# Moving each pair's last product behind two products of the next pair, in a decoder trunk on one Trainium2 core

## The chip, the core and the metric

The kernel runs on one NeuronCore of a Trainium2 chip. TensorE (PE) multiplies matrices: a weight load (PEld) puts 128x128 weights in place, a matmul then streams up to 512 columns past them, and the sums go to a bank of PSUM. VectorE (DVE) and ScalarE (ACT) do elementwise work, GpSimd (POOL) and SyncE (SP) here mostly start DMA transfers. Each engine works through its own instructions in order and waits for others by semaphores. The metric is the device time of one execution in microseconds (us); the time before is 2514.36 us, the median of 3 runs.

## What is computed

The reference is a trunk of two layers on 1024 rows of 1024 channels in float32. Each layer has a mixer (a state-space mixer in the first, an SSD mixer in the second) and a squared-ReLU MLP; the change lies in the MLPs alone.

```python
def _sq_relu_mlp(h, w1, w2):
    a = jax.nn.relu(h @ w1)
    return (a * a) @ w2

def reference(x, c, ...):
    cond = jax.nn.silu(c)
    for i in range(DEPTH):
        mod = cond @ ada_w[i] + ada_b[i]
        sh1, sc1, g1, sh2, sc2, g2 = jnp.split(mod[:, None, :], N_MOD, axis=-1)
        h = _modulate(_rmsnorm(x, norm_mix_g[i]), sh1, sc1)
        ...
        x = x + g1 * y
        h = _modulate(_rmsnorm(x, norm_mlp_g[i]), sh2, sc2)
        x = x + g2 * _sq_relu_mlp(h, mlp_w1[i], mlp_w2[i])
    return _rmsnorm(x, final_norm_g)
```

## The kernel before

**Precision.** Every float32 product is made of three matmuls. `split` (line 82) rounds a tile to a high part on ACT (line 84) and takes the rest on DVE (line 85). `mm3` (line 112) then issues high times high (line 117), high times low (118) and low times high (119). The split parts of weights are the tiles `whi` and `wlo`; `a` is those of one special tile, `a22`.

**First products (h @ w1).** They are done by a Strassen-like scheme with seven products of half the size. The 4096 outputs of w1 are taken as 16 pairs of 128-wide blocks (`of_pair`, line 457). The activations h lie split in seven panels: `b11`, `b21`, `b22`, `t1`, `t2`, `t3`, `t4`. In the trace the panel shows by the moving operand: `h0` to `h3` are `b11` or, with a trailing half of 1, `t1`; `h4` to `h7` are `b21` or `b22`; `t2`, `t3`, `t4` carry their names. One call of `product` (line 480) multiplies half a weight tile with a panel: four blocks of three matmuls, so 12 matmuls of 512 columns.

For 14 of the 16 pairs (`UPS`) two products, with `b11` and `b21`, are done ahead by `early` (line 515) while the panels for the rest are being made. Their results go to scratch in memory, `sscr` and `cscr`. The last two pairs do these two in place (`g.u0`).

**What one pair does.** `rows` (line 526) loads two raw weight tiles (line 95), splits the half of one into `a22`, forms four sums of halves in place (lines 534 to 537), and splits the two results into the units u1 and u2. `pair` (line 542) then runs, in the program's order:

- the loads of s and b12 from scratch (lines 554, 555);
- product `t2` with u1 into bank X, and `held` (line 490): s2 = s + X on DVE;
- product `t3` with u2 into bank W, and `held`: s7 = s + W;
- `ahead()`, which is `rows` of the next pair;
- product `t1` with u2, added in X; `act` (lines 497, 499, 500): b21 = relu(s7 + X)^2, and `put` stores it by a POOL DMA (line 506);
- product `t4` with `a22`, added in W; b22 = relu(s2 + W)^2, stored; `minus` (line 511) forms and stores t3;
- product `b22` with u1, added in X, the pair's last product; b11 = relu(s + X)^2, stored; then the three differences t1, t2, t4, stored.

**Buffers.** Temporaries of 512 columns (`tmp`, line 73: s, b12, s2, s7 and others) share six buffers. Raw weights share four (the pool `K.raw`; the gate's modulation rows, line 334, take from the same four in the first MLP). Split weights go round a ring of five (`unit_ring`, line 1473). `a22` has two, X four PSUM banks by turns, W three. `tt`, the result of `minus`, has four.

**What sets the order.** The program is written through a tile framework that places the semaphore waits and plans the order of each engine's instructions when the program is built; an earlier place in the program gives precedence. The trace therefore shows an order near the program's but not the same: matmuls of a later pair appear between products of an earlier one.

The loop over the pairs is in `mlp` (lines 1469 to 1497). It also advances `gates`, which in the first MLP computes the rows of one modulation (lines 333 and 334) at pairs 4 to 11. Behind the loop `mlp_down` (line 584) does the second products, whose first bank loads and splits are already planned among the last pairs.

Of the kernel before, what the change touches and what calls it, by code (L numbers as in the profile page):

```python
# [11 lines left out]
F32 = mybir.dt.float32  # L12
F32R = mybir.dt.float32r
I32 = mybir.dt.int32
AF = mybir.ActivationFunctionType
# [4 lines left out]
P = 128  # L20
D = 1024
L = 1024
HT = 512
# [3 lines left out]
UPS = 14  # L27
# [35 lines left out]

def psum(K):

    K.turn += 1
    i = K.turn % (6 if K.wide else 4)
    if i >= 4:
        return K.pw.tile([P, 512], F32, tag="pw", name="pd")
    return (K.ps if i < 2 or not K.psb else K.psb).tile([P, 512], F32, tag="ps", name="pd")  # L70


def psw(K):

    return K.pw.tile([P, 512], F32, tag="pw", name="pm")


def tmp(K, name):
    return K.tmp.tile([P, 512], F32, tag="t", bufs=6, name=name)


def split(K, hi, lo, src):

    K.nc.scalar.copy(hi, src)  # L84
    K.nc.vector.tensor_tensor(lo, src, hi.bitcast(F32), op=ALU.subtract)  # L85


def unit(K, src, n=1024):

    return unit_of(K, unit_raw(K, src, n), n)  # L90


def unit_raw(K, src, n=1024):
    raw = K.raw.tile([P, 1024], F32, tag="raw", name="raw")[:, 0:n]
    K.nc.sync.dma_start(raw, src)
    return raw


def unit_of(K, raw, n=1024):
    K.wturn = (K.wturn + 1) % len(K.wring)  # L100
    wt = K.wring[K.wturn]
    hi = wt.tile([P, 1024], F32R, tag="whi", name="whi")[:, 0:n]
    lo = wt.tile([P, 1024], F32R, tag="wlo", name="wlo")[:, 0:n]
    split(K, hi, lo, raw)
    return hi, lo


def unit_ring(K, *pools):

    K.wring, K.wturn = list(pools), -1  # L110
# [142 lines left out]
def h_new():  # L253
    return [[None, None] for _ in range(KT)]


def x_tiles(pool, order=range(KT)):
    x = h_new()
    for k in order:
        for f in range(2):  # L260
            x[k][f] = pool.tile([P, HT], F32, tag=f"x{k}{f}", name=f"x{k}{f}")
    return x
# [15 lines left out]
def drain(gen):  # L278
    for _ in gen:
        pass  # L280
# [56 lines left out]
def columns(K, rows, n):  # L337

    nc = K.nc
    row = K.wt.tile([P, 1024], F32, tag="whi", name="row")  # L340
    for f, r in enumerate(rows):
        nc.scalar.copy(row[0:1, half_of(f)], r[0:1])
    pt = pss(K)
    for j in range(n):
        nc.tensor.matmul(pt[:, j:j + 1], row[0:1, blk(j)], K.ones[0:1], start=True, stop=True)
    return pt
# [35 lines left out]
def modv(K, i, j):  # L382
    return K.mod[:, i * 48 + j * 8:i * 48 + j * 8 + 8]
# [73 lines left out]
def of_pair(m):  # L457

    i = m // 2 * 4 + m % 2
    return i, i + 2  # L460


class Up:
# [51 lines left out]
    def early(self, m, pan):  # L515

        nc = self.K.nc
        u0 = unit(self.K, self.w1[of_pair(m)[0]])
        X, Z = self.bank(m), self.second_bank()
        self.product(X, u0, 0, pan.b11, True)  # L520
        s1 = self.held(X, "s1")
        nc.gpsimd.dma_start(self.sscr[m], s1)
        self.product(Z, u0, HT, pan.b21, True)
        nc.gpsimd.dma_start(self.cscr[m], self.act(self.held(Z, "s1z", s1), None, True))

    def rows(self, m, pool, late):

        K, V, g = self.K, self.K.nc.vector, SimpleNamespace()
        r0, r1 = [unit_raw(K, self.w1[i]) for i in of_pair(m)]
        g.u0 = unit_of(K, r0) if late else None  # L530
        a22 = pool.tile([P, 1024], F32R, tag="br", name="a22", bufs=2)
        g.a22 = a22[:, 0:HT], a22[:, HT:]
        split(K, *g.a22, r1[:, HT:])
        V.tensor_tensor(r1[:, HT:], r1[:, 0:HT], r1[:, HT:], op=ALU.add)
        V.tensor_tensor(r1[:, 0:HT], r0[:, 0:HT], r1[:, 0:HT], op=ALU.subtract)
        V.tensor_tensor(r0[:, 0:HT], r1[:, HT:], r0[:, 0:HT], op=ALU.subtract)
        V.tensor_tensor(r0[:, HT:], r0[:, HT:], r0[:, 0:HT], op=ALU.subtract)
        g.u1 = unit_of(K, r0)
        g.u2 = unit_of(K, r1)
        return g  # L540

    def pair(self, m, g, pan, ahead):

        K = self.K
        X = self.bank(m)
        if g.u0:
            s = None
            self.product(X, g.u0, 0, pan.b11, True)
            b12 = self.held(X, "s1")
            Z = self.second_bank()  # L550
            self.product(Z, g.u0, HT, pan.b21, True)
        else:
            s, b12 = tmp(K, "s"), tmp(K, "b12")
            K.nc.sync.dma_start(s, self.sscr[m])
            K.nc.sync.dma_start(b12, self.cscr[m])
        self.product(X, g.u1, 0, pan.t2, not g.u0)
        s2 = self.held(X, "s2", s)
        W = self.second_bank()
        self.product(W, g.u2, 0, pan.t3, True)
        s7 = self.held(W, "s7", s)  # L560
        if g.u0:
            self.act(b12, Z)
        ahead()
        self.product(X, g.u2, HT, pan.t1, False)
        b21 = self.act(s7, X, not g.u0)
        self.put("b21", m, b21)
        self.product(W, g.a22, 0, pan.t4, False)
        b22 = self.act(s2, W, not g.u0)
        self.put("b22", m, b22)
        self.minus("t3", m, b22, b12)  # L570
        self.product(X, g.u1, HT, pan.b22, False)
        if s is None:
            b11 = tmp(K, "r")
            K.nc.scalar.activation(b11, X, AF.Relu)
            self.act(b11)
        else:
            b11 = self.act(s, X, True)
        self.put("b11", m, b11)
        t1 = self.minus("t1", m, b12, b11, b12)
        t2 = self.minus("t2", m, b22, t1)  # L580
        self.minus("t4", m, b21, t2)


def mlp_down(K, pool, x, bscr, w2, gate, xscr, mid, extra):
# [442 lines left out]
def s5_uproj(K, h, w):  # L1027

    nc = K.nc
    ahead = unit(K, w[0])  # L1030
    for m in range(KT):
        u = ahead
        if m < KT - 1:
            ahead = unit(K, w[m + 1])
        us = K.raw.tile([P, 1024], F32, tag="raw", name="us").rearrange("p (s c) -> p s c", s=8)
        for f in range(2):
            p = project(K, u, h, f)
            nc.scalar.copy(us[:, :, blk(f, 64)], p.rearrange("p (c s) -> p s c", s=8))
            if f == 0:
                yield  # L1040
        nc.scalar.dma_start(K.uscr[m], us)
        yield
# [385 lines left out]
def trunk(ctx: ExitStack, tc: tile.TileContext, io, out):  # L1428
    nc = tc.nc
    K = SimpleNamespace(nc=nc, tc=tc, io=io, turn=-1, psb=None, wide=False, adap=None, nada=2, nact=7)  # L1430
# [29 lines left out]
    def right(name, n=1):  # L1460
        return tc.alloc_tile_pool(name=name, bufs=n, side="right", reuse_waits="tile")
# [4 lines left out]
    def left(name, n=1):  # L1466
        return tc.alloc_tile_pool(name=name, bufs=n, reuse_waits="tile")

    def mlp(i, x, xa, up, pan, gate, mid, cond=None, mods=(), gates=()):

        mods, gates = iter(mods), iter(gates)
        K.wz = right("wz" + str(i), 2)
        unit_ring(K, K.wt, K.wt, K.wy, K.wz, K.wz)
        for t in ("whi", "wlo"):
            K.wz.tile([P, 1024], F32R, tag=t, name=t, bufs=2)
        rows = up.rows(0, K.wz, False)
        K.to = right("to" + str(i))
        for m in range(16):
            ahead = []
            up.pair(m, rows, pan, lambda: m < 15 and ahead.append(up.rows(m + 1, K.wz, m + 1 >= UPS)))  # L1480
            rows = ahead and ahead[0]
            if m >= 4:
                next(gates, None)
        K.to.release()
        K.tp.release()
        xl = left("xl" + str(i))
        x = x_tiles(xl)
        K.br = right("br" + str(i))
        K.adap = K.br if cond else None
        mlp_down(  # L1490
            K, K.br, x, K.bscr[i], io.w2[i], gate, K.hscr[i], lambda *a: mid(x, *a), lambda: next(mods, None)
        )
        drain(mods)
        K.adap = None
        K.br.release()
        K.wz.release()
        xl.release()
# [51 lines left out]
    g = h_new()  # L1549
    up = s5_uproj(K, h, io.s5_w_in)  # L1550
# [71 lines left out]
    up, mid = entry(0, x, K.G[:, 8:16], modv(K, 0, 3))  # L1622
# [11 lines left out]
    def mid(x, f, bank, order):  # L1634
        G, sh = K.G[:, 16:24], modv(K, 1, 0)

        def each(k, pb):
            h1[k][f] = (h_tile(K, k, f, 0), h_tile(K, k, f, 1))
            norm_tile(K, x[k][f], h1[k][f], pb, G[:, k:k + 1], sh[:, k:k + 1])
            nc.gpsimd.dma_start(K.rscr[k, :, half_of(f)], x[k][f])  # L1640

        return norm_steps(K, x, f, each, bank, order)

    mlp(0, x, xa, up, up.pan, modv(K, 0, 5), mid, True, mod1, gate0)
    cond.release()
    K.wx = left("wx1", 2)
# [8 lines left out]
    t1 = right("tab1")  # L1655
# [24 lines left out]
    up, mid = entry(1, x1, K.G[:, 24:32], modv(K, 1, 3))  # L1680
# [126 lines left out]
```

## Time and profile before

| what | us |
|---|---|
| median of 3 runs (2514.31 to 2516.89) | 2514.36 |
| span of the profiled execution | 2516.1 |
| PE busy in the span | 2445.6 |
| DVE busy in the span | 1913.1 |
| first MLP: from the first product t2 of pair 0 to the end of the pairs | 529 to 775 |
| second MLP: the same | 1942 to 2188 |

The page of the profile gives busy time by engine, the chain that ended last (the work that led to the end, followed back from releaser to releaser) and the costliest groups. Views of the trace give the same for a stretch: busy time by stretch, waits by pairs of engines and lines, the chain piece by piece, and single instructions in order of time. In those rows "px" is bank X of a pair, "pv" is bank W or the bank of an early product, and a bracket says how long the engine was idle before the instruction and what ended it.

### The profile page before, as it was taken

How to read it: one execution, taken by the hardware profiler on the slowest of the kernel's cores; microseconds unless marked ns; L12 is line 12 of the kernel's file. 1: busy time of each engine (PE TensorE's matmuls, PEld its weight loads, DVE VectorE, ACT ScalarE, POOL GpSimd, SP SyncE). 2: the span in 40 equal slices, each digit the busy share in tenths (PEclk: the TensorE clock that was granted, in tenths of full speed). 3: DMA queues.
4: the chain of work that ended last, by engine and by line, in shares of the span. 5: the costliest groups of instructions: out<-in, count | busy, mean ns of one | idle time of the engine just before them, and what ended most of it. 6: DMA issues, size and time to landing. Idle time of an engine off the chain costs nothing.

```text
span 2516.1 us, 32759 instructions
## 1 busy us (share of the span) xinstructions
PE 2445.6 (97%) x11624; PEld 1961.2 (78%) x11624; DVE 1913.1 (76%) x3265; ACT 1167.4 (46%) x1975; POOL 214.4 (9%) x400
## 2 busy tenths in 40 slices
PE   7999899999999999999999999999999999999997
PEld 3788788877777778877887878877888777788886
DVE  8798754978887898968585867789687777787664
ACT  4577412744444334534464645534246444444342
POOL 0010000122221000100000000000011222210000
PEclk8999999999999999999999999999999999999998
DMA  6576773467769999823554554574246666794752
GB/s 244 149 174 165 237 251 97 148 205 258 263 226 318 322 307 320 276 85 109 162 160 153 159 168 145 180 249 141 80 137 210 217 223 222 256 318 150 252 191 84
DMA packets 284643, 503.80 MB, mean 200 GB/s; under 512 B 22080, under 2 KB 162368, under 8 KB 284480
## 3 DMA queue, kind: packets, MB, share of 16 engines
q1 hardware_dynamic: 242496, 386.34, 47.8%
q0 software_dynamic: 32384, 106.98, 12.5%
q10 hardware_dynamic: 9600, 8.39, 1.0%
q8 instruction: 91, 1.49, 0.2%
q14 instruction: 72, 0.59, 0.1%
HBM read 364.27 MB, written 133.17 MB: 198 GB/s over the span
## 4 chain that ended last, share of the span: by engine, by line
PE 80%; DVE 7%; DMA 5%; ACT 3%; issue 2%; DVEq 0%; SPq 0%; ACTq 0%
PE pd L117 11%; PE pd L118 11%; PE pd L119 11%; PE py L117 4%; PE py L119 4%; PE py L118 4%; PE px L117 4%; PE px L119 3%; PE px L118 3%; PE pv L117 3%; PE pv L118 3%; PE pv L119 3%; PE pm L119 2%; PE pm L117 2%; PE pm L118 2%
## 5 line engine op out<-in xcount | busy, mean ns | idle before, releaser
L84 ACT CAST whi<-raw 128x1024 fp32r<-128x1024 f32 x241 | 251.0, 1047 | 360.5 <-PE pd L118 145.4
L85 DVE TENSOR_TENSOR wlo<-raw,whi 128x1024 fp32r<-128x1024 f32 x241 | 293.0, 1217 | 107.8 <-ACT whi L84 104.2
L334 DVE SCALAR_TENSOR_TENSOR ada<-ada,cond 128x1024 f32<-128x1024 f32 x88 | 107.0, 1220 | 57.6 <-DMA ada<-in_ada 57.3
L499 ACT ACTIVATE s<-s 128x512 f32<-128x512 f32 x84 | 53.0, 631 | 156.1 <-DVE s L497 153.6
L391 POOL DMA_DIRECT2D hscr<-x x32 | 17.4, 543 | 955.4 <-DVE x L758 752.5
L1257 DVE SCALAR_TENSOR_TENSOR cacc<-cr,conv,cacc 128x1024 f32<-128x1024 f32 x72 | 91.7, 1277 | 1.0 <-ACT cacc L1238 0.6
L1310 ACT ACTIVATE L<-csb,cs 128x128 f32<-128x128 f32 x224 | 69.9, 390 | 39.8 <-DMA csb<-csr 39.8
L506 POOL DMA_DIRECT2D b<-s x96 | 52.0, 542 | 319.9 <-ACT s L500 278.5
L497 DVE TENSOR_TENSOR s<-s,px 128x512 f32<-128x512 f32 x60 | 41.0, 683 | 34.4 <-PE px L119 34.4
L497 DVE TENSOR_TENSOR s<-s,pv 128x512 f32<-128x512 f32 x36 | 24.7, 686 | 55.1 <-PE pv L119 55.1
L506 POOL DMA_DIRECT2D b<-tt x96 | 52.0, 542 | 44.8 <-DVE tt L511 27.9
L500 ACT ACTIVATE s<-s 128x512 f32<-128x512 f32 x84 | 53.2, 633 | 2.7
L1261 ACT ACTIVATE cth<-cacc 128x512 f32<-128x512 f32 x48 | 27.7, 624 | 42.3 <-DVE cacc L1257 40.4
L673 DVE SCALAR_TENSOR_TENSOR x<-py,mod,x 128x512 f32<-128x512 f32 x40 | 27.6, 743 | 24.4 <-PE py L119 24.4
L209 ACT ACTIVATE sq<-x 128x512 f32<-128x512 f32 x28 | 16.7, 625 | 54.1 <-DVE x L673 49.1
L1330 DVE SCALAR_TENSOR_TENSOR y<-xs,cst,pm 128x128 f32<-128x128 f32 x128 | 38.2, 340 | 4.7 <-PE pm L1327 4.7
L117 PE MATMUL pd<-h00h,whi 128*128 128x512 f32 (+1 forms) x97 | 39.9, 413 | 1.8 <-ACT h00h L238 1.8
L1237 ACT COPY cr<-pd 128x512 f32<-128x512 f32 x48 | 27.8, 579 | 28.8 <-PE pd L119 28.8
L1128 ACT ACTIVATE gt<-pd,bgh 128x512 f32<-128x512 f32 x16 | 11.0, 685 | 63.9 <-PE pd L119 63.9
L117 PE MATMUL pd<-h01h,whi 128*128 128x512 f32 x97 | 39.5, 407 | 0.5 <-DVE h61h L758 0.5
L119 PE MATMUL pd<-h10h,wlo 128*128 128x512 f32 (+1 forms) x97 | 39.3, 405 | 0.0
L118 PE MATMUL pd<-h30l,whi 128*128 128x512 f32 (+1 forms) x97 | 38.9, 401 | 0.0
(1006 smaller groups left out, 8165.1 us busy)
## 6 DMA issues: line engine op xcount, KB each, us to landing
raw<-in_w SPq DMA_DIRECT2D x204, 512.0 KB, 4.7
br<-b SPq DMA_DIRECT2D x112, 512.0 KB, 5.4
ada<-in_ada SPq DMA_DIRECT2D x96, 512.0 KB, 5.3
b<-s POOLq DMA_DIRECT2D x96, 256.0 KB, 2.9
b<-tt POOLq DMA_DIRECT2D x96, 256.0 KB, 3.8
csb<-csr SPq DMA_DIRECT2D x32, 512.0 KB, 4.6
raw<-in_w_xbc SPq DMA_DIRECT2D x24, 512.0 KB, 4.3
xscr<-cacc SPq DMA_DIRECT2D x24, 512.0 KB, 2.7
```

The costliest lines, as they stand in the source:

```text
L84: K.nc.scalar.copy(hi, src)
L85: K.nc.vector.tensor_tensor(lo, src, hi.bitcast(F32), op=ALU.subtract)
L117: K.nc.tensor.matmul(ps, wh, xh, start=start and i == 0, stop=False, skip_group_check=more)
L118: K.nc.tensor.matmul(ps, wh, xl, start=False, stop=False, skip_group_check=more)
L119: K.nc.tensor.matmul(ps, wl, xh, start=False, stop=stop and i == n - 1, skip_group_check=more)
L334: K.nc.vector.scalar_tensor_tensor(r, r, 1.0, K.cond, op0=ALU.mult, op1=ALU.mult, accum_out=acc)
L497: nc.vector.tensor_tensor(t, t, p, op=ALU.add)
L499: nc.scalar.activation(t, t, AF.Relu)
L500: nc.scalar.activation(t, t, AF.Square)
L506: self.K.nc.gpsimd.dma_start(self.bscr[DOWN.index(nm)][m // 2][m % 2], t)
L1257: V.scalar_tensor_tensor(acc, cr[:, t:t + L], K.cw[:, i, t:t + 1], acc, op0=ALU.mult, op1=ALU.add)
L1310: nc.scalar.activation(Lm[:, r, :], cb[:, r, :], AF.Relu, bias=S.cs[:, c0 + r:c0 + r + 1], scale=-1.0)
```

## The change

The work of a pair is cut into `sums`, `units`, `begin`, `middle`, `last` and `finish`, and the loop runs 17 times, with the pair `now`, the pair before it, `done`, and the pair behind it, `ahead`:

- the raw loads, the split of `a22` and the sums of `ahead` stand at the head (for the last two pairs also the split of u0);
- then `begin` of `now`: products `t2` and `t3`, with s loaded before them;
- then `last` of `done`: its product `b22`;
- then the splits u1, u2 of `ahead`, then `finish` of `done`: b11, t1, t2, t4;
- then `middle` of `now`: the load of b12, products `t1` and `t4`, b21, b22 and t3.

The tile b12 that is loaded, and the tile r of the last two pairs, come from two buffers of their own in the pool `K.to`, and no longer from the six temporaries. In the last two pairs the bank of the product `b21` is taken before the product `b11` is issued.

```diff
-    def rows(self, m, pool, late):
+    def sums(self, m, pool, late):
 
-        K, V, g = self.K, self.K.nc.vector, SimpleNamespace()
-        r0, r1 = [unit_raw(K, self.w1[i]) for i in of_pair(m)]
+        K, V, g = self.K, self.K.nc.vector, SimpleNamespace(m=m)
+        r0, r1 = g.raws = [unit_raw(K, self.w1[i]) for i in of_pair(m)]
         g.u0 = unit_of(K, r0) if late else None
...
         V.tensor_tensor(r0[:, HT:], r0[:, HT:], r0[:, 0:HT], op=ALU.subtract)
-        g.u1 = unit_of(K, r0)
-        g.u2 = unit_of(K, r1)
         return g
+    def units(self, g):
+
+        g.u1 = unit_of(self.K, g.raws[0])
+        g.u2 = unit_of(self.K, g.raws[1])
+
+    def begin(self, g, pan):
+
+        K, m = self.K, g.m
+        g.X = self.bank(m)
         if g.u0:
-            s = None
-            self.product(X, g.u0, 0, pan.b11, True)
-            b12 = self.held(X, "s1")
-            Z = self.second_bank()
+            g.s, Z = None, self.second_bank()
+            self.product(g.X, g.u0, 0, pan.b11, True)
+            g.b12 = self.held(g.X, "s1")
             self.product(Z, g.u0, HT, pan.b21, True)
         else:
-            s, b12 = tmp(K, "s"), tmp(K, "b12")
-            K.nc.sync.dma_start(s, self.sscr[m])
-            K.nc.sync.dma_start(b12, self.cscr[m])
+            g.s = tmp(K, "s")
+            K.nc.sync.dma_start(g.s, self.sscr[m])
...
+    def middle(self, g, pan):
+
+        K, m = self.K, g.m
+        if not g.u0:
+            g.b12 = self.K.to.tile([P, HT], F32, tag="b12", name="b12", bufs=2)
+            K.nc.sync.dma_start(g.b12, self.cscr[m])
+        self.product(g.X, g.u2, HT, pan.t1, False)
+        g.b21 = self.act(g.s7, g.X, not g.u0)
+        self.put("b21", m, g.b21)
+        self.product(g.W, g.a22, 0, pan.t4, False)
+        g.b22 = self.act(g.s2, g.W, not g.u0)
+        self.put("b22", m, g.b22)
+        self.minus("t3", m, g.b22, g.b12)
+
+    def last(self, g, pan):
+
+        self.product(g.X, g.u1, HT, pan.b22, False)
+
+    def finish(self, g):
+
+        K, m = self.K, g.m
+        if g.s is None:
+            b11 = K.to.tile([P, HT], F32, tag="b12", name="r", bufs=2)
+            K.nc.scalar.activation(b11, g.X, AF.Relu)
             self.act(b11)
         else:
-            b11 = self.act(s, X, True)
+            b11 = self.act(g.s, g.X, True)
...
-        for m in range(16):
-            ahead = []
-            up.pair(m, rows, pan, lambda: m < 15 and ahead.append(up.rows(m + 1, K.wz, m + 1 >= UPS)))
-            rows = ahead and ahead[0]
+        for m in range(17):
+            ahead = up.sums(m + 1, K.wz, m + 1 >= UPS) if m < 15 else None
+            if now:
+                up.begin(now, pan)
+            if done:
+                up.last(done, pan)
+            if ahead:
+                up.units(ahead)
+            if done:
+                up.finish(done)
+            if now:
+                up.middle(now, pan)
             if m >= 4:
                 next(gates, None)
+            now, done = ahead, now
```

More of the change, by code (lines that the diff above doesn't have):

```diff
@@ L537, in rows @@
         V.tensor_tensor(r0[:, HT:], r0[:, HT:], r0[:, 0:HT], op=ALU.subtract)
-        g.u1 = unit_of(K, r0)
-        g.u2 = unit_of(K, r1)
-        return g
-    def pair(self, m, g, pan, ahead):
-        K = self.K
-        X = self.bank(m)
+        return g
+    def units(self, g):
[4 more added lines that the diff above has]
+        g.X = self.bank(m)
         if g.u0:
-            s = None
-            self.product(X, g.u0, 0, pan.b11, True)
-            b12 = self.held(X, "s1")
-            Z = self.second_bank()
+            g.s, Z = None, self.second_bank()
+            self.product(g.X, g.u0, 0, pan.b11, True)
+            g.b12 = self.held(g.X, "s1")
@@ L551, in pair @@
             self.product(Z, g.u0, HT, pan.b21, True)
         else:
-            s, b12 = tmp(K, "s"), tmp(K, "b12")
-            K.nc.sync.dma_start(s, self.sscr[m])
-            K.nc.sync.dma_start(b12, self.cscr[m])
[L556 to L560, printed above, removed]
-        if g.u0:
-            self.act(b12, Z)
-        ahead()
-        self.product(X, g.u2, HT, pan.t1, False)
@@ L565, in pair @@
[L565 to L574, printed above, removed]
+            g.s = tmp(K, "s")
+            K.nc.sync.dma_start(g.s, self.sscr[m])
+        self.product(g.X, g.u1, 0, pan.t2, not g.u0)
@@ new lines, in begin @@
+        g.s2 = self.held(g.X, "s2", g.s)
+        g.W = self.second_bank()
+        self.product(g.W, g.u2, 0, pan.t3, True)
+        g.s7 = self.held(g.W, "s7", g.s)
+        if g.u0:
+            self.act(g.b12, Z)
+    def middle(self, g, pan):
[10 more added lines that the diff above has]
+        self.minus("t3", m, g.b22, g.b12)
@@ L575, in pair @@
+    def last(self, g, pan):
[5 more added lines that the diff above has]
+            K.nc.scalar.activation(b11, g.X, AF.Relu)
             self.act(b11)
         else:
-            b11 = self.act(s, X, True)
+            b11 = self.act(g.s, g.X, True)
         self.put("b11", m, b11)
-        t1 = self.minus("t1", m, b12, b11, b12)
-        t2 = self.minus("t2", m, b22, t1)
@@ L581, in pair @@
-        self.minus("t4", m, b21, t2)
+        t1 = self.minus("t1", m, g.b12, b11, g.b12)
+        t2 = self.minus("t2", m, g.b22, t1)
+        self.minus("t4", m, g.b21, t2)
 def mlp_down(K, pool, x, bscr, w2, gate, xscr, mid, extra):
@@ L1475, in mlp @@
             K.wz.tile([P, 1024], F32R, tag=t, name=t, bufs=2)
-        rows = up.rows(0, K.wz, False)
+        now, done = up.sums(0, K.wz, False), None
+        up.units(now)
         K.to = right("to" + str(i))
-        for m in range(16):
-            ahead = []
-            up.pair(m, rows, pan, lambda: m < 15 and ahead.append(up.rows(m + 1, K.wz, m + 1 >= UPS)))
-            rows = ahead and ahead[0]
+        for m in range(17):
[10 more added lines that the diff above has]
+                up.middle(now, pan)
             if m >= 4:
                 next(gates, None)
+            now, done = ahead, now
         K.to.release()
```

## The prediction

> **What bounds the kernel now.** I read the busy shares on the page first, then the chain that ended last.
>
> ```profile
> span 2516.1 us, 32759 instructions
> PE 2445.6 (97%) x11624; PEld 1961.2 (78%) x11624; DVE 1913.1 (76%) x3265; ACT 1167.4 (46%) x1975; POOL 214.4 (9%) x400
> PE 80%; DVE 7%; DMA 5%; ACT 3%; issue 2%; DVEq 0%; SPq 0%; ACTq 0%
> ```
>
> TensorE (PE) is the bound of the whole, and the change takes no matmul away. So only time in which PE stands still inside the two stages of first products can be won. I looked for it with busy times by stretch: per MLP, a stretch in the middle of the pairs and one at the late pairs, where the order of work is different.
>
> ```profile
> 551.04:716.25 165.21, 160.66 (x675) 124.69 (x674) 134.50 (x195) 70.89 (x100) 41.70 (x77) 1.00 0.75 253
> 726.87:764.30 37.43, 37.43 (x164) 30.56 (x163) 26.89 (x38) 14.20 (x22) 9.75 (x18) 1.00 0.68 237
> 1962.10:2129.00 166.90, 162.33 (x677) 126.00 (x676) 125.63 (x178) 71.53 (x100) 41.74 (x78) 0.99 0.66 226
> 2139.50:2177.00 37.50, 37.50 (x165) 30.58 (x164) 27.40 (x40) 15.14 (x23) 9.75 (x18) 1.00 0.70 241
> ```
>
> After the length stand busy time and instruction count of PE, weight load, VectorE (DVE), ScalarE (ACT) and GpSimd, then clock, DMA share and GB/s. In the late stretches PE has no idle time: 37.43 us for 163 matmuls (one is counted at both edges), 0.2296 us each. In the middle stretch of the first MLP, 674 matmuls take 165.21 us, 0.2451 each; in the second about 675 take 166.90, 0.2473. At the late pace they would take 154.8 and 155.0. So 10.4 us and 11.9 us are lost there. A pair is 60 matmuls: 14.7 to 14.8 us now, 13.8 at the unstalled pace.
>
> Who makes PE wait? The chain of waits, read through one pair, answers:
>
> ```profile
> 617.30 0.70 DVE s L497
> 618.02 0.64 ACT s L499
> 618.68 0.64 ACT s L500
> 619.96 0.70 DVE raw L535
> 621.73 0.54 ACT s L499
> 622.29 0.64 ACT s L500
> 622.96 0.04 DVE b L511
> 624.17 0.69 DVE tt L511
> 625.50 0.69 DVE s L490
> 626.23 0.50 PE px L117
> ```
>
> These are the pieces of the chain between two stretches of PE. At 617.30 DVE picks up product t4 of a pair. Then come its ReLU and square (L499, L500), weight sums in between (L535), the ReLU and square of the last product, the two differences t1 and t2 (L511), and only then `held` of the next pair (L490), which reads bank X so that product t1 may write it at 626.23. That is 8.93 us in which PE has only b22, t2 and t3 to do, 3 x 2.76 = 8.27 us. The rest is a wait or a few matmuls of the following pair. The same chain starts again at 632.11 and ends at 641.10, 8.99 us. So the period is not PE's: products t1 and t4 (5.5) plus about 9.0 of chain make 14.5, and with the clumsy start of each product 14.7 to 14.8.
>
> The direct waits of PE in the same stretch, and those at the ends of the stages:
>
> ```profile
> PE px L117 <- ACT whi L84: 2.4, 3, 1.4
> PE pv L119 <- DVE wlo L85: 0.9, 3, 0.3
> PE pv L117 <- ACT whi L84: 0.9, 4, 0.2
> ...
> 536.06 0.50 PE L117 MATMUL px<-h01h,whi 128*128 128x512 f32 x1 [1.31 <-DVE s L490]
> 766.59 0.50 PE L117 MATMUL px<-h01h,whi 128*128 128x512 f32 x1 [1.80 <-ACT s L488]
> 1947.79 0.50 PE L117 MATMUL px<-h01h,whi 128*128 128x512 f32 x1 [0.49 <-DVE s L490]
> 2179.60 0.50 PE L117 MATMUL px<-h01h,whi 128*128 128x512 f32 x1 [1.59 <-ACT s L488]
> ```
>
> The three sums are 4.2 us; they end on a split weight (whi, wlo), because while t1 is blocked PE's queue goes on with matmuls of a pair whose weights are only just being split. The four rows are the first pair's t1 (waits on s) and the last pair's t1 (waits on a copy that stands behind splits of the next stage in ACT's queue).
>
> **The change, part by part.** No product, VectorE operation, activation or transfer is added or taken away; order, two buffers and the place of one load change.
>
> *Last product behind two of the next pair.* PE's order becomes t2, t3 of pair m+1, then b22 of m, then t1, t4 of m+1. Let T be the end of t4 of pair m. `held` s2 still has its input at T+2.8, but t1 of m+1 now starts at T+8.3 rather than T+5.5, and s2 no longer stands behind ReLU, square, t1 and t2 of pair m, for these come after T+8.3. The chain from t4's pick-up to s2 is cut: what is left ahead of s2 on DVE is the add of b22, one split of 512, four sums and t3, seven operations. By the row of L490 below each is about 0.68, so 4.8 us; s2 ends at about T+5.5, 2.8 us before it is needed. Gain up to the whole 10.4 + 11.9 = 22.3 us.
>
> *The last pair.* Between t3 and t1 of pair 15 now lies b22 of pair 14, 2.76 us, more than the waits of 1.80 and 1.59. Gain up to 3.4 us. Behind the last t4 nothing changes: b22 of pair 15 follows, as now.
>
> *The first pair.* t1 of pair 0 has no last product ahead of it; 1.31 and 0.49 stay, cost and gain nothing.
>
> *Sums at the head, splits later.* The sums of m+2 cannot start before T either way, for the a22 tile has two buffers and t4 of pair m reads one. The split of u1 can run from about T+5.5 and is needed at T+13.8. The ring has five weight buffers, so the split of u2 takes the one that u1 of pair m held, which will be read until T+8.3 instead of T+2.8. ScalarE (1.05) and DVE (1.22, row below) finish it at about T+10.6; it is needed at T+16.6. Cost nothing, cover 6 us; with the cover gone each us late is one us per pair.
>
> *DVE as the next bound.* 134.50 us busy in 674/60 = 11.2 pairs is 12.0 per pair, 11.2 in the second MLP, against 13.8: 87% and 81%. It can hold the pace, if its waits stay below 1.8 us per pair.
>
> *s from six buffers, b12 from two of its own.* Now a pair takes four of the six temporary buffers, and after the change three, but for two pairs at once: all six. s of m+1 can be fetched only when pair m-1 has ended its differences. The rows of this load:
>
> ```profile
> SPq L554 <- DMA b<-s: 36.6, 8, 5.1
> ...
> s<-sscr SPq DMA_DIRECT2D x11, 256.0 KB, 3.9
> ...
> DMA to landing us min/median/max: 2.7/3.8/6.4
> ...
> 627.87 0.33 SPq L554 DMA_DIRECT2D s<-sscr  x1
> 640.36 0.69 DVE s L490
> ...
> L85 DVE TENSOR_TENSOR wlo<-raw,whi 128x1024 fp32r<-128x1024 f32 x23 | 28.0, 1219 | 0.2 <-ACT whi L84 0.2
> L490 DVE TENSOR_TENSOR s<-s,pv 128x512 f32<-128x512 f32 x12 | 8.2, 679 | 0.0
> ```
>
> Today s is asked for 12.5 us ahead of its use. After the change: b22 of m-1 ends 8.3 us after t4 of m-1. In the chain above b22 ends at about 617.3 + 2.76 = 620.1 and the difference t2 at 624.86, 4.8 later, so 13.1; 3.9 to land and 0.7 for s2 make 17.7. Product t1 of m+1 starts 13.8 + 8.3 = 22.1 after the same point. So 4.4 us are over. The same sum as a period: (13.1 + wait of SP's queue + landing + 0.7 + 5.5) / 2, which is 11.6 with the median landing and no wait, below PE's 13.8. Bounds: no wait and 2.7 costs nothing; wait 5.1 and landing 6.4 give 15.4 a pair. I take no cost: the median is nearer by far. Behind s on SP's queue stand the raw weights, whose readers wait until T of the next pair, and b12, needed at the end of t4; none is near.
>
> *What is left.* A fixed order never meets its inputs exactly. The 4.2 us of short waits on whi and wlo in 11.2 pairs are 0.38 per pair; their kind (a matmul queued ahead of its weights) need not go with the chain. I leave 0.4 per pair standing: bounds are nothing and, if PE is then held up as often as by all causes now, 10.4/11.2 = 0.9. So 22.4 x 0.4 = 9 us.
>
> **Sum.** 22.3 + 3.4 - 9 = 16.7, say 17 us. The profiled execution of 2516.1 would become 2499; the median of the runs shown, 2514.4, lies 1.7 below that span, so I carry the difference over: 2514.4 - 17 = 2497.4.
>
> One rule bears on 1.4 us of this sum:
>
> ```profile
> 653.35 0.50 PE L117 MATMUL px<-t20h,whi 128*128 128x512 f32 x1 [1.37 <-ACT whi L84]
> 2065.05 0.50 PE L117 MATMUL px<-t20h,whi 128*128 128x512 f32 x1 [1.37 <-ACT whi L84]
> ...
> 2066.90:2070.20 3.30, 3.30 (x10) 2.51 (x8) 2.54 (x4) 0.00 (x0) 0.54 (x1) 0.52 0.91 269
> ```
>
> The same wait of 1.37 us stands in both MLPs; behind the second one the granted clock was 0.52 for 3.3 us, in which some 8 matmuls ran where 14 fit, 1.4 us. I count it as won, for the wait ahead of it goes. The Trainium skill, "TensorE: Matmul & The Clock Gate", section "HAM oscillation — how this bites in real kernels", names idle gaps over about 3.4 us as what throttles PE. By it a gap of 1.37 would not be the cause, the slow stretch could stay, and the time would be 1.4 us longer, 2498.8. The trace has one case for each view, so it does not decide.
>
> **The rivals.** (1) *The gain is real but eaten on the way*: DVE at 87% stands in a fixed order, and s, now fetched late, blocks what is behind it (sums, splits, adds). If 2 us of waits per pair come upon 12.0, the first MLP stays at 14.0 to 14.7, and only the second and the ends gain: 3.4 + some 3, or nothing. Time 2510 to 2516. For it: every spare buffer is used up. Against it: 4.4 us of slack, and DVE waits today mostly for PE.
>
> (2) *Slower: the fetch of s becomes the period.* Place: SP's queue at L554 and s2 on DVE. By the formula above it overtakes PE when wait plus landing pass 8.3 us, and today's 14.75 when they pass 10.2. At the worst rows, 11.5, the period is 15.4: 22.4 x 0.65 = 14.6 us lost, less 3.4, gives 2526. For it: such a wait of up to 5.1 is in the trace today, 8 times. Against it: it ends with the landing of a store of an s tile, whereas the first buffer to come free, that of t2, needs no landing.
>
> (3) *The change doesn't do what it says.* PE's order in the trace is not that of the program:
>
> ```profile
> 640.32 0.43 PE L117 MATMUL px<-t20h,whi 128*128 128x512 f32 x1
> ...
> 641.10 0.50 PE L117 MATMUL px<-h01h,whi 128*128 128x512 f32 x1
> ```
>
> Matmuls of t2 of the pair after next run ahead of t1, as the order of each engine is planned when the program is built. The planner could place the last product first wherever the weights of the next pair are late in its plan. Then nothing is cut and the time is 2514, within 0.2%.
>
> **How the numbers follow.** Forecast 0.72; rival 1 0.13; rival 2 0.08; rival 3 0.07. A difference of 0.2%, 5 us, is about what a measurement of this kernel can tell from no change. Faster by more: the forecast, and a third of rival 1, 0.76. Within: the rest of rival 1 and rival 3, 0.16. Slower: 0.08. The forecast's own ends are no leftover waits (2514.4 - 25.7 = 2488.7) and 0.9 a pair with the ends alone won (2511). Outside 2488 to 2511 lie rivals 2 and 3 and a part of rival 1, about 2 in 10, so that is the range too.
>
> **What would show it.** Right: the stretch of pairs at 13.8 to 14.2 us per 60 matmuls; b22 of a pair between t3 and t1 of the next; no wait of t1 on L488 at the last pair, but still one at the first; the chain through these stages nearly all PE. Wrong: L490 on DVE waiting for s<-sscr pair after pair (rival 2, and 1 if DVE's queue is then full); b22 still ahead of t2 (rival 3); PE waiting for whi of u2 behind the last product, where I gave 6 us of cover. A slow clock elsewhere, or another order of work in the second products, would make the total wrong with the stages right.

## The result, and the profile after

| kernel | median, us | runs | ratio to before (95% interval) |
|---|---|---|---|
| before | 2514.65 | 4 (2514.31 to 2516.89) | |
| changed | 2494.72 | 4 (2490.01 to 2497.53) | 0.9919 (0.9905 to 0.9933) |

The change makes the kernel 20 us faster; 17 were forecast (2497.4, range 2488 to 2511). The profiled execution of the changed kernel has a span of 2494.2 us. Its page says little of where the time went:

```profile
span 2494.2 us, 32748 instructions
PE 2433.9 (98%) x11624; PEld 1961.2 (79%) x11624; DVE 1916.7 (77%) x3265; ACT 1169.3 (47%) x1975; POOL 214.4 (9%) x400
```

Work is as it was: 11624 matmuls, 3265 VectorE instructions. I cut each trace at the first and the last matmul of each stage, which gives the time by stage in us ("to pairs" ends where the first product t2 of pair 0 begins):

| stage | before | changed |
|---|---|---|
| to the pairs of the first MLP | 529.1 | 527.9 |
| first products, first MLP | 245.8 | 238.7 |
| second products, first MLP | 323.0 | 324.6 |
| between | 843.7 | 843.2 |
| first products, second MLP | 246.3 | 233.0 |
| second products, second MLP | 310.0 | 309.7 |
| tail | 18.0 | 17.2 |

The second MLP's first products gave 13.3 us, the first MLP's only 7.1. Busy times by stretch in the middle of the pairs (columns as before) show the difference:

```profile
541.87:719.02 177.15, 174.26 (x750) 139.87 (x748) 149.00 (x215) 78.92 (x111) 46.59 (x86) 1.00 0.75 257
1948.50:2120.50 172.00, 172.00 (x748) 140.40 (x747) 143.35 (x200) 79.88 (x111) 46.55 (x86) 1.00 0.71 244
```

In the second MLP PE has no idle time left: 172.00 us for 747 matmuls, 0.2303 each, 13.8 us a pair. In the first it loses 177.15 - 749 x 0.2303 = 4.7 us. The waits of PE from the first pair to the end of that stage are of one kind now, and VectorE's waits in the pairs name what is behind them (who waited, for whom: us in all, times, the longest):

```profile
PE px L117 <- DVE s L490: 3.8, 6, 0.9
```

```profile
DVE s L490 <- DMA s<-sscr: 6.6, 5, 3.1
```

All six are product t1 waiting for `held` s2 (one of them at pair 0), and s2 waits for the fetch of s: in each of the six the trace has s landing 0.12 or 0.13 us before s2 starts. The short waits on split weights (whi, wlo) are gone.

### The profile page after: what moved, and what is told of

Its sections match the earlier page's. It is cut to its first block, busy times and chain, and to the rows that moved or that the text cites. A ratio compares the mean times of both kernels' runs of the same rounds, so it can differ in the third digit from the quotient of the medians.

```text
span 2494.2 us, 32748 instructions
## 1 busy us (share of the span) xinstructions
PE 2433.9 (98%) x11624; PEld 1961.2 (79%) x11624; DVE 1916.7 (77%) x3265; ACT 1169.3 (47%) x1975; POOL 214.4 (9%) x400
## 4 chain that ended last, share of the span: by engine, by line
PE 67%; issue 15%; DMA 6%; DVE 4%; POOL 3%; ACT 2%; POOLq 0%; SPq 0%; DVEq 0%; ACTq 0%
PE pd L117 9%; PE pd L118 9%; PE pd L119 9%; PE py L118 4%; PE py L119 4%; PE py L117 4%; DMA ada<-in_ada 3%; PE px L117 2%; PE px L119 2%; PE px L118 2%; PE pm L117 2%; POOL b L506 2%; PE pm L118 2%; PE pm L119 2%; PE pv L117 2%
## 5 line engine op out<-in xcount | busy, mean ns | idle before, releaser
L687 DVE SCALAR_TENSOR_TENSOR x<-py,mod,x 128x512 f32<-128x512 f32 x40 | 27.8, 745 | 24.5 <-PE py L119 24.5
L511 DVE TENSOR_TENSOR tt<-s,b 128x512 f32<-128x512 f32 x56 | 38.7, 690 | 0.8
```

## What the experiments were to decide

The prediction gave the gain to the order: s2 of the next pair no longer stands behind the last product and its differences. The rival is in the same diff. b12 and r left the six temporaries, so a pair holds three and not four. Before the change, when s2 of pair k+1 is due, pair k still holds s, b12, s2 and s7 (by then s, s2 and s7 have become b11, b22 and b21 in place), and pair k+1 holds s and b12. That is all six, and s2 can only be written once the difference t2 of pair k is done with b22. Either reason gives the same chain of waits.

## Experiments

### e1: the old order with the new buffers

```diff
-            s, b12 = tmp(K, "s"), tmp(K, "b12")
+            s = tmp(K, "s")
+            b12 = K.to.tile([P, HT], F32, tag="b12", name="b12", bufs=2)
...
-            b11 = tmp(K, "r")
+            b11 = K.to.tile([P, HT], F32, tag="b12", name="r", bufs=2)
```

> The kernel before, with b12 and r of the last pairs taken from two buffers of their own in K.to, so that a pair holds three of the six temporaries and not four; the order is the old one. Theory (order): s2 of the next pair stands behind ReLU, square and the differences of the last product because these come earlier in the program, and PE has only three products to cover them; buffers alone leave the stages of first products at 243 to 247 us (245.6 and 246.1 before), the time within 5 us of 2514.7. Rival (buffers): s2 waited for the temporary that the difference t2 frees; with it free the stages fall by 8 us or more each, the time to 2500 or less.

Measured: 2490.92 us (2489.84 to 2492.01), ratio 0.9904 (0.9887 to 0.9920). The theory fell and the rival holds: two buffers, nothing moved, bring all of the gain. The stages of first products take 235.0 and 234.0 us. The stretches of pairs have no idle time in either MLP:

```profile
542.00:707.50 165.50, 165.50 (x721) 135.18 (x720) 144.60 (x210) 77.81 (x109) 45.52 (x84) 1.00 0.78 270
1940.50:2106.00 165.50, 165.50 (x720) 135.22 (x719) 135.35 (x194) 78.00 (x109) 45.49 (x84) 1.00 0.71 246
```

Single instructions of VectorE in order of time show what the buffer does, first before the change, then in e1:

```profile
622.96 0.69 DVE L511 TENSOR_TENSOR b<-b,s 128x512 f32<-128x512 f32 x1
...
624.17 0.68 DVE L511 TENSOR_TENSOR tt<-s,b 128x512 f32<-128x512 f32 x1
624.89 0.69 DVE L511 TENSOR_TENSOR tt<-s,tt 128x512 f32<-128x512 f32 x1
625.50 0.68 DVE L490 TENSOR_TENSOR s<-s,px 128x512 f32<-128x512 f32 x1
```

```profile
643.18 0.69 DVE L511 TENSOR_TENSOR b<-b,s 128x512 f32<-128x512 f32 x1
643.79 0.68 DVE L490 TENSOR_TENSOR s<-s,px 128x512 f32<-128x512 f32 x1
644.39 0.68 DVE L511 TENSOR_TENSOR tt<-s,b 128x512 f32<-128x512 f32 x1
...
646.13 0.68 DVE L511 TENSOR_TENSOR tt<-s,tt 128x512 f32<-128x512 f32 x1
```

s2 (L490) now runs ahead of the difference t2 (644.39) and of t4 (646.13). Before the change it came behind both, t2 at 624.17, t4 at 624.89 and s2 at 625.50. It still stands behind the last product, its ReLU and t1. What it gains is about 1.3 us, from the start of t2 to that of s2 before the change, and the chain was less than that too long: a pair took 14.7 to 14.8 us against 13.8.

### e8: the old order, the new buffers, and two temporaries taken away

```diff
+        up.kept = [tmp(K, "kept") for _ in range(2)]
+        for t in up.kept:
+            K.nc.vector.memset(t[:, 0:1], 0.0)
         for m in range(16):
...
         self.put("b11", m, b11)
+        if m == 13:
+            for t in self.kept:
+                K.nc.vector.tensor_tensor(t[:, 0:1], t[:, 0:1], b11[:, 0:1], op=ALU.add)
```

> The old order with b12 in two buffers of its own (e1), but two of the six temporaries are kept by two tiles that nothing uses, from the head of the pairs to pair 13. A pair holds three, so with s of the next pair all four are taken, and s2 of the next pair has to wait for the temporary that the difference t2 frees, as in the kernel before. Theory (buffers): the stages go back from 235 and 234 to 243 to 250 us, the time to 2508 to 2522. Rival (what e1 won came from a freer SP queue or from b12's stores elsewhere, not from the temporaries): the stages stay below 238, the time below 2500.

Measured: 2512.62 us (2510.1 to 2516.58), ratio 0.9998 (0.9988 to 1.0007). Everything that e1 won is gone; the stages take 246.9 and 244.1 us. VectorE's order and the waits of PE in the pairs are those of before:

```profile
621.50 0.69 DVE L511 TENSOR_TENSOR tt<-s,b 128x512 f32<-128x512 f32 x1
622.22 0.69 DVE L511 TENSOR_TENSOR tt<-s,tt 128x512 f32<-128x512 f32 x1
622.83 0.68 DVE L490 TENSOR_TENSOR s<-s,px 128x512 f32<-128x512 f32 x1
```

```profile
PE px L117 <- ACT whi L84: 2.6, 3, 1.4
PE pv L119 <- DVE wlo L85: 0.9, 3, 0.3
PE pv L117 <- ACT whi L84: 0.9, 4, 0.2
```

s2 is back behind t2 and t4, and the three waits come back with nearly the same sums (2.4, 0.9 and 0.9 before). So the waits on split weights were a consequence as well: they come and go with the temporaries. (That PE's plan, with t1 blocked, pulls matmuls forward whose weights are only being split fits the rows, and was not tested by itself.) e1 and e8 together settle the cause: it is the number of free temporaries.

The converse, the new order with b12 among the six, was not run. Two pairs in flight would then want up to seven of the six, so by this count the order needs the buffers; no run shows what it does without them.

### e2 and e3: where the sums and the splits stand

e2 puts the sums behind `begin`, e3 the splits at the head:

```diff
-            ahead = up.sums(m + 1, K.wz, m + 1 >= UPS) if m < 15 else None
             if now:
                 up.begin(now, pan)
+            ahead = up.sums(m + 1, K.wz, m + 1 >= UPS) if m < 15 else None
```

```diff
             ahead = up.sums(m + 1, K.wz, m + 1 >= UPS) if m < 15 else None
+            if ahead:
+                up.units(ahead)
             if now:
                 up.begin(now, pan)
             if done:
                 up.last(done, pan)
-            if ahead:
-                up.units(ahead)
```

> The changed kernel with the sums of the next pair put behind products t2 and t3 in the program, not at the head; the last product stays behind them, the splits behind it. Theory (the last product's place is what counts): stages stay within 3 us of 238.5 and 232.8, the time within 0.2% of 2494.7. Rival (the sums at the head carry a part): sums get later than s2 and s7 on VectorE, splits become late, and the second stage grows by 4 us or more.

> The changed kernel with the splits u1, u2 of the next pair put at the head, right behind the sums. Theory: the split of u2 waits for the last product in any case, as it takes over u1's buffer of that pair, and has 6 us of cover; the second stage stays at 232 to 236 us, the time within 0.2% of 2494.7. Rival (the later splits carry a part): the split of u1 goes ahead of s2 and s7 on VectorE and delays t1 and t4; a stage grows by 5 us or more.

Measured: 2493.83 us (ratio 0.9915, 0.9900 to 0.9929) and 2496.82 us (0.9928, 0.9913 to 0.9943). Stages 238.3 and 233.2 in e2, 239.7 and 232.2 in e3. Both stay within the spread of the changed kernel, and the second stage within 1 us of its own. These two parts of the change do nothing that can be measured.

### e4: the fetch of s twice

```diff
             K.nc.sync.dma_start(g.s, self.sscr[m])
+            K.nc.sync.dma_start(g.s, self.sscr[m])
```

> The changed kernel with the fetch of s issued twice into the same tile, one behind the other, which doubles its time (about 5 us more). Theory of the prediction (a loop over two pairs with 4.4 us to spare): the second stage stays at 233 to 236 us. Rival (a loop over one pair: s2 waits in VectorE's queue, so the pick-up of the last product, the differences and the next fetch are late too; some 12 us long in the second stage, 14.3 to 15 in the first): the second stage goes to 15 us a pair or more, by 20 us or more, and the first grows likewise; the kernel ends slower than before.

Measured: 2586.99 us, ratio 1.0290 (1.0274 to 1.0305); stages 286.7 and 276.9 us. The loop over two pairs with 4.4 us to spare, on which the prediction took the late fetch to be free, is refuted. One turn of the real loop stands here in the order of time of VectorE and SP's queue, with the next s2 as its last row:

```profile
2059.83 0.69 DVE L490 TENSOR_TENSOR s<-s,px 128x512 f32<-128x512 f32 x1 [5.09 <-DMA s<-sscr]
2063.37 0.68 DVE L497 TENSOR_TENSOR s<-s,px 128x512 f32<-128x512 f32 x1
2066.14 0.69 DVE L511 TENSOR_TENSOR tt<-s,b 128x512 f32<-128x512 f32 x1
2066.86 0.33 SPq L556 DMA_DIRECT2D s<-sscr  x1
2073.15 0.32 SPq L557 DMA_DIRECT2D s<-sscr  x1
2076.87 0.69 DVE L490 TENSOR_TENSOR s<-s,px 128x512 f32<-128x512 f32 x1 [4.22 <-DMA s<-sscr]
```

While s2 waits, a sum, s7, a split and the add of the last product (2063.37) stand behind it in VectorE's queue. So the difference t2 (2066.14) comes late, and with it the temporary into which the next s is fetched (2066.86, and again 2073.15). The turn takes 17.04 us, and it is one pair, not two. From the issue of the first fetch to s2 it is 10.0 us; with that in place of the landing the prediction's formula gives only about 14.7 us a pair. The granted clock was lower as well, 0.93 and 0.95 over the two stages against 1.00 in the changed kernel, so part of what PE lost there is slow matmuls and not waits. The turn shown does not hang on that: in it VectorE waits for no product.

### e5 to e7 and e9: the waits that are left in the first MLP

The same loop runs in the changed kernel in the first MLP, in the rows of VectorE, SP's queue and PE:

```profile
659.79 0.69 DVE L490 TENSOR_TENSOR s<-s,px 128x512 f32<-128x512 f32 x1 [1.27 <-DMA b<-s]
664.07 0.68 DVE L497 TENSOR_TENSOR s<-s,px 128x512 f32<-128x512 f32 x1
666.84 0.69 DVE L511 TENSOR_TENSOR tt<-s,b 128x512 f32<-128x512 f32 x1
667.56 0.33 SPq L556 DMA_DIRECT2D s<-sscr  x1
674.68 0.69 DVE L490 TENSOR_TENSOR s<-s,px 128x512 f32<-128x512 f32 x1 [1.54 <-PE px L119]
675.42 0.50 PE L117 MATMUL px<-h01h,whi 128*128 128x512 f32 x1 [0.76 <-DVE s L490]
```

One turn is 14.89 us against PE's 13.8, of which 7.1 are from the issue of the fetch to s2. The profile puts the wait at 674.68 down to PE, but the last matmul of product t2 had started at 668.75; s is the other input, and it landed 7.0 us after its issue, 0.12 us before s2. The row at 659.79 is put down to a store, but there too s had landed only 0.12 us before. Three edits test this, beside a second set of runs of the changed kernel. e6 gives s of the odd pairs a buffer of its own, e9 gives one to s2 of the odd pairs; both pay with one of the four buffers tt. e7 takes the modulation rows out of the pairs.

```diff
-            g.s = tmp(K, "s")
+            g.s = self.K.to.tile([P, HT], F32, tag="s", name="s", bufs=1) if m % 2 else tmp(K, "s")
```

```diff
-        mods, gates = iter(mods), iter(gates)
+        mods = (s for g in (gates, mods) for s in g)
...
-            if m >= 4:
-                next(gates, None)
```

```diff
-        g.s2 = self.held(g.X, "s2", g.s)
+        own = K.to.tile([P, HT], F32, tag="s2", name="s2", bufs=1) if m % 2 else None
+        g.s2 = self.held(g.X, "s2", g.s, own)
```

> The changed kernel unaltered, as the measure for the next two on the same chip. 2490 to 2498, stages 235 to 239 and 232 to 234 us.

> The changed kernel with a seventh buffer: s of the odd pairs comes from one of its own in K.to, paid with one of the four buffers tt. Two pairs then hold five temporaries, and s can be fetched a pair ahead. Theory (the waits that are left in the first stage come from the late fetch of s): they go, the first stage falls from 238.5 to 234 or 235 us, the second stays at 233, the time falls by 3 to 5 us. Rival (they come from VectorE's load of 12 us and more per pair with the modulation rows): the first stage stays at 237 to 239.

> The changed kernel with the eight modulation rows of pairs 4 to 11 of the first MLP moved into the second products, ahead of the rows that are computed there. Theory (late fetch of s): without these loads of 512 KB the fetch lands as soon as in the second MLP, and without their products VectorE reaches the differences sooner, so the first stage comes near the second, 233 to 235 us; what the rows cost behind it is seen in the total. Rival (the first MLP's stage is held up by something else than the rows): it stays at 237 to 239.

> The changed kernel with s2 of the odd pairs in a buffer of its own, paid with one of the four buffers tt. s2 of an odd pair is free again before the next odd one needs it, so here the seventh buffer really leaves one temporary over for the fetch of s (in e6 the own buffer of s came free only with the store of b11, later than today). Theory (late fetch of s holds up the first stage): the first stage falls from 238.5 to 240 down to 233 to 236, the second stays at 232 to 234. Rival (three buffers tt are too few, and that was what cost e6 its time): the first stage stays at 240 or above.

| kernel | median, us | ratio (95% interval) | first MLP's stage | second MLP's |
|---|---|---|---|---|
| e5 | 2496.73 (2492.84 to 2502.94) | 0.9921 (0.9904 to 0.9937) | 240.5 | 232.2 |
| e6 | 2508.66 | 0.9972 (0.9963 to 0.9982) | 245.6 | 236.0 |
| e7 | 2495.56 | 0.9924 (0.9909 to 0.9939) | 234.0 | 232.2 |
| e9 | 2490.69 | 0.9915 (0.9898 to 0.9931) | 233.8 | 232.9 |

e6 went the wrong way, and the edit was at fault: s becomes b11, so its one buffer comes free only when that has been stored, later than the temporary that t2 frees. SP's queue shows the wait, and VectorE passes it on, in the pairs of the first MLP:

```profile
SPq L556 <- DMA b<-s: 28.4, 6, 5.8
```

```profile
DVE s L490 <- DMA s<-sscr: 18.3, 6, 4.4
```

It is one more sign of the loop, in the other direction. In e9 a temporary is really left over. The fetch of s lands in 4.5 us (median in the pairs, 5.9 in the changed kernel), behind pair 0 no s2 waits for it, and the first stage falls to 233.8 us; three buffers tt are enough. In e7 the stage falls just as far: without the rows the loop stays below PE's pace, as in the second MLP. The fetch lands in 5.5 us (median), and not in the 5.0 of the second MLP as was expected, so the gain is likely in the main from VectorE's shorter work. Its total gains nothing that can be measured (2495.56 against 2496.73), because the second products take 328.4 us instead of 324.6; the rows have moved there.

### e10 and e11: the new order for the last pair alone

e10 is the changed kernel with another loop: pairs 0 to 13 in the old order, and only pair 14's last product behind two products of pair 15. e11 is e1 again, on the same chip.

```diff
         for m in range(17):
-            ahead = up.sums(m + 1, K.wz, m + 1 >= UPS) if m < 15 else None
             if now:
                 up.begin(now, pan)
             if done:
                 up.last(done, pan)
+            ahead = up.sums(m + 1, K.wz, m + 1 >= UPS) if m < 15 else None
             if ahead:
                 up.units(ahead)
             if done:
                 up.finish(done)
             if now:
                 up.middle(now, pan)
+            if now and m < 14:
+                up.last(now, pan)
+                up.finish(now)
+                now = None
```

> Old order in pairs 0 to 13 with b12 in its own buffers; only pair 14's last product is put behind two products of pair 15. Theory: the steady pairs run without waits as in e1, and the wait at the last t1 (1.2 and 1.9 us in e1) goes as in the changed kernel, so about 3 us less than e1: 2486 to 2490. Rival: the last pair's place makes no difference to the sum, as the stage behind it waits for the same loads: 2490 to 2492.

> e1 once more, unaltered, beside the one above on the same chip: 2489 to 2493 us, stages 234 to 236 and 233 to 235 us.

Measured: e10 2490.63 us (ratio 0.9911, 0.9897 to 0.9926), e11 2491.44 (0.9916, 0.9902 to 0.9931); they cannot be told apart. The waits of PE over the whole first stage, first in e1, then in e10:

```profile
PE px L117 <- DVE s L490: 1.4, 1, 1.4
PE px L117 <- ACT s L488: 1.0, 1, 1.0
```

```profile
PE px L117 <- DVE s L490: 0.9, 1, 0.9
```

The wait at the last pair is gone, and so are 1.8 us of the first stage (233.2 against 235.0), and 1.9 of the second (232.1 against 234.0); e11 has 235.2 and 235.5. But the first MLP's second products take 324.2 us in e10 and 320.2 in e1. From 780 to 895 us PE waits there for splits, first in the changed kernel, then in e1:

```profile
PE py L118 <- DVE h41l L85: 4.9, 1, 4.9
PE pm L118 <- DVE h41l L85: 2.0, 1, 2.0
```

```profile
PE py L119 <- DVE wlo L85: 2.8, 1, 2.8
PE pm L119 <- DVE wlo L85: 2.5, 2, 1.6
```

The longest wait comes from VectorE's order. In the changed kernel the split that makes h41l stands behind eight additions to x (L687); in e1 it stands ahead of them (there L674):

```profile
871.13 4.04 DVE L687 SCALAR_TENSOR_TENSOR x<-pm,mod,x 128x512 f32<-128x512 f32 x6
875.08 1.40 DVE L687 SCALAR_TENSOR_TENSOR x<-pn,mod,x 128x512 f32<-128x512 f32 x2
...
877.00 0.69 DVE L85 TENSOR_TENSOR h41l<-br,h41h 128x512 fp32r<-128x512 f32 x1
```

```profile
865.52 0.68 DVE L85 TENSOR_TENSOR h41l<-br,h41h 128x512 fp32r<-128x512 f32 x1
...
866.73 4.04 DVE L674 SCALAR_TENSOR_TENSOR x<-pm,mod,x 128x512 f32<-128x512 f32 x6
```

e10 has the order of the changed kernel, and a wait of 5.0 us. All waits of this window sum to 9.4 us in the changed kernel and 6.2 in e1, and from about the end of the longest one the granted clock is 0.50 for 6.8 us there (876.7 to 883.5) and for 3.4 in e1 (873.1 to 876.5). The order there is planned anew for each kernel. Why the plan behind the new order's end is the worse one stays open.

e1 and its repeat e11, e9 and e10, all at 2490.6 to 2491.4, are the fastest by their medians. But the medians come from different chips; by the ratios, each to runs of the kernel before that were taken beside it, the lead over the changed kernel is 1 to 4 us. The intervals overlap, so it is not shown.

## Why the prediction was right, and where it was not

**What bounds the kernel.** Right: the pairs ran at the pace of the chain and not of PE, and with the chain shortened they run at 13.8 us a pair in the second MLP, as the late stretch of before had it. In the first they take 14.2 (177.15 us for 749 matmuls).

**"Last product behind two of the next pair … Gain up to the whole 10.4 + 11.9 = 22.3 us".** This is the step that failed, in its reason and not in its size. The gain came with the edit but not from the order: e1 has it without any move, and e8 loses it to two kept buffers. I read "s2 behind the differences" as a place in a queue. It was a wait for a temporary; the list of the live ones, which I counted only for the kernel after, holds six of six for the kernel before. The Trainium skill, "Perfetto Trace Analysis", section "Optimization Strategy", says of the same gap that comes again and again on the engine that should be busy that it can mean too little memory for the next tile. By e1 and e8 this case agrees, with a gap of 0.6 us or less of PE in most pairs.

**"The last pair … Gain up to 3.4 us".** Right in kind: the waits of 1.80 and 1.59 are gone from the changed kernel but for 0.15 us at 758.1. e1 against e10 puts the move at 1.8 and 1.9 us of the stages, and in the first MLP it was given back behind them. The waits at the first pair stay, 0.90 and 0.59 us, as forecast.

**"Sums at the head, splits later … Cost nothing".** Right by e2 and e3.

**"s from six buffers … I take no cost".** Mis-sized: the first MLP pays about 5 us (238.7 against 233.8 in e9), the second none. The period formula was wrong by its two pairs. A late s2 holds up the pick-up of the pair before it in the same queue, so the loop closes within one pair. That is rival 1's mechanism, at a smaller price than the rival had; rival 2's formula is refuted by e4. The sign that the prediction gave for both, L490 waiting for s<-sscr pair after pair, did show in the first MLP.

**"I leave 0.4 per pair standing", 9 us.** The second MLP has nothing left in its pairs, the first 4.7 us, from s and not from the planning of weights. Two errors of opposite sign, no cost for s and 9 us for the plan, brought the sum near the truth; that is luck.

**The clock.** The slow stretch of the second MLP is gone with the wait ahead of it. In e8, where the wait is back, a slow stretch stands behind it in the first MLP, where before had none:

```profile
650.69 0.50 PE L117 MATMUL px<-t20h,whi 128*128 128x512 f32 x1 [1.36 <-ACT whi L84]
```

```profile
652.60:655.60 3.00, 3.00 (x8) 2.33 (x8) 2.48 (x4) 0.00 (x0) 0.54 (x1) 0.52 0.97 284
```

So it came out as I counted it. By the gaps over about 3.4 us of the Trainium skill, "TensorE: Matmul & The Clock Gate", section "HAM oscillation — how this bites in real kernels", it need not have gone; the rows here, with slow stretches behind gaps of 1.36 and 1.37 us, do not agree with that bound. That such a wait brings a slow stretch on, some of the time, is likely, as none of the stretches of pairs without waits has one, and it is not shown: in e5 waits of PE of 2.0 us at 536.4 and 1.2 us at 663.1 had none behind them. The timing is not explained.

## What to carry to other kernels

When an instruction stands behind the end of the work before it, count the live tiles of its pool at that moment before taking it for a matter of order; keeping a buffer or two occupied on purpose tells the two apart in one run. Where work is overlapped over two stages, every fetch into a shared pool is tied to the release of the stage before: look for a loop that closes through one engine's queue, and not only for the data's own path. When a change brings order and buffers together, run each alone, for the part that was meant may be the one that costs.

## What the runs showed that I had not expected

A fetch of 256 KB more per pair, with nothing else changed, made the kernel 92 us slower than the changed one (2586.99 against 2494.72), over 3 us a pair for 14 pairs in both MLPs, though the DMA engines were busy for 0.65 of the first MLP's pairs only. The granted clock over those pairs was 0.92. And in the traces of before and of e8 a wait of under 1.4 us was followed by some 3 us at about half the granted clock (0.52), at different places.
